# Booking GpSimd's transfers on the bus and shifting ranks by a seeded table, in the planner of a two-layer decoder kernel

## The chip, the cores and the metric

The kernel runs on one core of a Trainium2 chip. The metric is the time of one execution in microseconds (us), measured on the device. Engines are named as in the profile: PE (TensorE, matrix products), PEld (its weight loads), DVE (VectorE), ACT (ScalarE), POOL (GpSimd) and SP (SyncE, which only issues transfers here).

## The reference

Two decoder layers on 256 tokens of width 1024, all float32. Each layer has sparse attention with three branches (8 heads, 2 of keys and values) beside forgetting attention (8 heads), one output product for both, and a squared-ReLU MLP of width 4096; the norms stand before and after each half.

```python
def reference(x, w_in, ..., g_post_mlp):
    for l in range(DEPTH):                                   # 2
        h = _rms_norm(x, g_pre_mix[l])
        parts = jnp.split(h @ w_in[l], split_at, axis=-1)    # 1024 x 2848
...
        o_nsa = _nsa_mixer(...)      # compressed, selected and window branch, gated
        o_fox = _fox_mixer(...)      # softmax with summed log-sigmoid decay
        mix = jnp.concatenate([o_nsa, o_fox], axis=-1) @ w_out[l]
        x = x + _rms_norm(mix, g_post_mix[l])
        h = _rms_norm(x, g_pre_mlp[l])
        y = jnp.square(jax.nn.relu(h @ w_up[l])) @ w_down[l]
        x = x + _rms_norm(y, g_post_mlp[l])
    return x
```

## The kernel before

**Products.** A float32 product is made of three products in the rounded type float32r: both operands are split into a high part and a rest, and high·high, high·low and low·high are summed in PSUM (`mm3`). Activations lie transposed in `xT`, `aT` or `aS`. Weights come from memory in units of mostly 512 KB, and there are two ways for them. A *split* unit is loaded by SP into `wraw` (`Weights.load`, a ring of nine); ACT copies it into `whi`, and DVE subtracts `whi` from `wraw` into `wlo` (`Weights.get`; the two rings hold seven each). A *cast* unit, every second unit of `w_up` from the second column block on, 14 in a layer, goes round DVE (`Weights.cast`): a GpSimd transfer loads it rounded into the first half of a slot of `whic`, ACT writes the negative of that into the second half (`whic<-whic` in the profile), and a second GpSimd transfer adds the unrounded weights to it, which leaves the rest. The ring `whic` has three slots, so a first load waits until PE has done with the slot's former content; `CAST_LEAD` places the load 14 units ahead.

**The MLP.** Up products go to PSUM tiles `s`, 256 columns of outputs at a time; ACT and DVE make `h` of them (`h<-s`, `h<-s,h`), square and split them. Down products are made for pairs of units by a scheme of seven block products in place of eight (`Weights.pair`): DVE builds sums of weight blocks (`wsum`), which are split like weights, and seven PSUM banks (`o`, `acc`, `x`, `s`) gather the block products of thirteen pairs. Then the banks are combined once (`acc<-acc,s1`, `x<-x,s1` and so on, on DVE and ACT), and the last units are added in the plain way. At the end of a half `sandwich` normalises the result, adds it to the residual `x0` or `x1` (tokens 0 to 127 and 128 to 255), and where another product follows makes the next operand: `mg` on DVE, four PE transposes for each 512 columns (`s<-cst,mg`, `cst` holds the identity), and `xT<-s,xT` on DVE.

**What sets the order.** No engine call is made at once. A `Recorder` takes the 4876 operations with their buffers and dependences (`Recorder.add`), and a planner, `Recorder.schedule` (L325), replays them on a model of the five engines. Whenever an engine of the model is free it takes, of the operations that are ready and whose buffers are free, the one with the lowest `rank`; urgent ones go first, and two rules keep small fp32 matmuls of PE together. Ranks start as the position in the program (`key`; loads and splits have that of an earlier unit). `order` (L297) goes through four stages, the attention and the MLP of each layer, which begin at operations 0, 1095, 2464 and 3523. In each it plans, gives every operation off PE the due time that the plan's PE order sets it (`deadlines`, L269), plans again, up to four times from two starts, and keeps the ranks of the shortest plan. The order of the last plan is the order in which `emit` (L434) issues the instructions; each engine's queue then runs in that order and waits on semaphores. All instructions therefore carry the line L441 in the profile (L486 after the change).

The model's costs are nanoseconds. A transfer by SP occupies `bus` at 360 bytes per ns, and ends 900 ns after its bytes; some have an allowance on top. A GpSimd transfer does not touch `bus`: it occupies GpSimd for 1200 ns (`_cost`, L485), and what depends on it may start 5000 ns after that (`_latency`, L460).

Of the kernel before, what the change touches and what calls it, by code (L numbers as in the profile page):

```python
# [24 lines left out]
P = 128  # L25
# [8 lines left out]
LASTK = 4  # L34
LANE = 0.9
PASSES = 4
LANDING = 2500.0

SLACK, LATE = {"vector": 20, "scalar": 20}, 2000
# [146 lines left out]

class Op:
    __slots__ = ("small", "engine", "name", "args", "kw", "key", "urgent", "cost", "deps", "succs", "bufs",
                 "missing", "ready", "start", "end", "tile", "rank")


class Recorder:
# [21 lines left out]
    def add(self, engine, name, args, kw):  # L214
        if self.group is not None:
            assert engine == "tensor"
            self.group.append((name, args, kw))
            return
        op = Op()
        op.engine, op.name, op.args, op.kw = engine, name, args, kw  # L220
        op.key = len(self.ops) if self.key is None else self.key
        if self.lane is not None and self.key is None:
            op.key = self.lane + LANE * (len(self.ops) - self.lane)
        op.urgent = self.hot
        views = []
        for _, a, k in args[2] if name == "stretch" else [(name, args, kw)]:
            views += [(i == 0, v) for i, v in enumerate(a) if isinstance(v, View)]
            views += [(i in ("out", "accum_out"), v) for i, v in k.items() if isinstance(v, View)]
        op.tile = _tile(op) if engine == "tensor" else None
        op.small = engine == "tensor" and not any(v.buf.name.startswith(("whi", "wlo")) for _, v in views)  # L230
        op.cost = _cost(op, views) + SLACK.get(engine, 0)
        deps = {} if self.after is None else {self.after: -1e9}
        op.bufs = []
        for is_out, v in sorted(views, key=lambda x: x[0]):
            b, m = v.buf, v.mask()
            if b not in op.bufs:
                op.bufs.append(b)

            def against(entries):
                for o, p, q, bank in entries:  # L240
                    if o is not op and o not in deps and (
                            (bank and engine == "tensor") or
                            (p[0] < v.p[1] and v.p[0] < p[1] and (m & q).any())):
                        deps[o] = _latency(o, op)

            against(b.writes)
            entry = (op, v.p, m, is_out and b.psum and engine == "tensor")
            if is_out:
                against(b.reads)
                b.writes = [w for w in b.writes if not (  # L250
                    w[0] in deps and v.p[0] <= w[1][0] and w[1][1] <= v.p[1] and not (w[2] & ~m).any())]
                b.writes.append(entry)
            else:
                if b.psum:
                    for o, _, _, _ in b.reads:
                        if o.engine != engine and o is not op and o not in deps:
                            deps[o] = 130.0
                b.reads.append(entry)
        op.deps = deps
        for b in op.bufs:  # L260
            if not b.ops:
                self.fifo.setdefault(b.tag, []).append(b)
            b.ops += 1
        op.succs = []
        for d in deps:
            d.succs.append(op)
        self.ops.append(op)

    def deadlines(self, out):  # L269
# [14 lines left out]
        for op in reversed(out):  # L284
            d = due.get(op, t)
            cost = op.cost + LANDING if op.engine == "sync" else op.cost
            for x in op.succs:
# [9 lines left out]
    def order(self):  # L297

        for op in self.ops:
            op.rank = op.key
        done = 0
        for bound in self.stages + [len(self.ops)]:
            rest = self.ops[done:]
            best = None
            for first in ([op.rank for op in rest], [op.key for op in rest]):
                for op, rank in zip(rest, first):
                    op.rank = rank
                for i in range(PASSES + 1):  # L310
                    if i:
                        kept = [op.rank for op in self.ops[:done]]
                        self.deadlines(out)
                        for op, rank in zip(self.ops, kept):
                            op.rank = rank
                    out = self.schedule()
                    end = max(op.end for op in out)
                    if best is None or end < best[0]:
                        best = end, [op.rank for op in rest]
            for op, rank in zip(rest, best[1]):  # L320
                op.rank = rank
            done = bound
        return self.schedule()

    def schedule(self):  # L325

# [9 lines left out]
        busy = dict.fromkeys(waiting, 0.0)  # L336
        bus, tiled, loads = 0.0, (P, P), 0
# [29 lines left out]
        while events:  # L367
            t, _, released = heapq.heappop(events)
# [4 lines left out]
            for e, ops in waiting.items():  # L373
                while busy[e] <= t:
                    best = None
                    for op in ops:
                        if op.ready <= t and (best is None or (best.urgent, -best.rank) < (op.urgent, -op.rank)) and fits(op):
                            best = op
                    if best is None:
                        break  # L380
                    if e == "tensor" and best.small and not small_last and not best.urgent and t < best.ready + HOLD:
                        more = [op for op in ops if op.ready <= t and fits(op)]
                        if sum(op.small for op in more) < 2:
                            best = min((op for op in more if not op.small), key=lambda op: op.rank, default=best)
                    if e == "tensor" and small_last and not best.urgent and not best.small:
                        more = [op for op in ops if op.small and op.ready <= t and op.rank < best.rank + REACH and fits(op)]
                        best = min(more, key=lambda op: op.rank, default=best)
# [15 lines left out]
                    if e == "sync":  # L403
                        busy[e] = t + 450
                        bus = max(bus, t + 1150) + best.cost + RAMP.get(loads, 0)
                        best.end = bus + 900 + (LATE if loads >= len(FIRSTS) else 0)
                        loads += 1
                    else:
                        busy[e] = best.end = t + best.cost
                        small_last = best.small if e == "tensor" else small_last  # L410
                        if e == "tensor" and best.tile != tiled:
                            busy[e] = best.end = best.end + (tiled == (P, P)) * ENTER + (tiled != (P, P)) * LEAVE
                            tiled = best.tile
# [39 lines left out]
def _tile(op):  # L453

    up = lambda n: next(m for m in (32, 64, P) if n <= m)
    lhsT = op.args[1]
    return (P, P) if op.name == "transpose" else (up(lhsT.shape[0]), up(int(np.prod(lhsT.shape[1:]))))


def _latency(a, b):  # L460
    if a.engine == "sync":
        return 50.0
    if a.name == "dma_start":
        return 5000.0
    if a.engine == b.engine == "tensor":
        return 0.0
    if a.engine == "tensor":
        return 360.0 if b.name == "tensor_tensor_reduce" else 200.0
    if b.engine == "tensor":
        return 260.0 if a.engine == "vector" else 230.0  # L470
    return 130.0 if a.engine == "vector" else 145.0
# [13 lines left out]
def _cost(op, views):  # L485

    out = op.args[0] if op.args else op.kw["out"]
    n = int(np.prod(out.shape[1:]))
    part = 100 * (out.shape[0] < P)
    if op.engine == "gpsimd":  # L490
        if op.name == "dma_start":
            return 1200.0
        return 200 + 0.72 * n + 10 * int(np.prod(out.shape[1:-1]))
    if op.engine == "sync":
        v = views[0][1]
        return v.shape[0] * int(np.prod(v.shape[1:])) * 4 / 360.0
    if op.engine == "tensor":
        if op.name == "stretch":
            side = P // min(op.tile)
            return sum(_product(*x[:2], side) for x in op.args[2][::side])  # L500
        return _product(op.name, op.args, 1)
    if op.engine == "vector":
        if op.name == "reciprocal":
            return 60 + 6.5 * n
        if op.name == "tensor_reduce":
            n = int(np.prod(op.args[1].shape[1:]))
        fast = op.name in ("tensor_copy", "tensor_scalar", "memset") and not any(v.buf.psum for _, v in views)
        aps = sum(isinstance(v, View) for v in op.args[2:4]) if op.name == "tensor_scalar" else int(
            op.name == "scalar_tensor_tensor" and isinstance(op.args[2], View))
        return 68 + part + 64 * aps + n * (0.52 if fast else 1.04) + 10 * (op.name == "tensor_tensor_reduce")  # L510
    src = op.args[1]
    aps = sum(isinstance(op.kw.get(k), View) for k in ("bias", "scale", "accum_out"))
    return n / 1.2 + (55 if src.buf.psum else 92) + 93 * aps
# [1282 lines left out]
```

## Time and profile before

| | us |
|---|---|
| three runs | 610.91, 609.5, 611.77 |
| their median | 610.91 |
| the profiled execution | 606.49 |
| its span, first to last instruction | 604.7 |

The profiled execution is one of its own; 1.8 us of it lie outside the span. TensorE's granted clock was 0.997 of full speed in it. The rows of the page and of the timeline that carry the argument stand in the prediction. In a row of a group, the number behind the bar is the busy time, then the mean ns of one, then the idle time of that engine just ahead of them and what ended most of it.

### The profile page before, as it was taken

How to read it: one execution, taken by the hardware profiler on the slowest of the kernel's cores; microseconds unless marked ns; L12 is line 12 of the kernel's file. 1: busy time of each engine (PE TensorE's matmuls, PEld its weight loads, DVE VectorE, ACT ScalarE, POOL GpSimd, SP SyncE). 2: the span in 40 equal slices, each digit the busy share in tenths (PEclk: the TensorE clock that was granted, in tenths of full speed). 3: DMA queues.
4: the chain of work that ended last, by engine and by line, in shares of the span. 5: the costliest groups of instructions: out<-in, count | busy, mean ns of one | idle time of the engine just before them, and what ended most of it. 6: DMA issues, size and time to landing. Idle time of an engine off the chain costs nothing.

```text
span 604.7 us, 9793 instructions
## 1 busy us (share of the span) xinstructions
PE 595.4 (98%) x3322; PEld 494.7 (82%) x3322; DVE 550.6 (91%) x1187; ACT 449.3 (74%) x862; POOL 49.5 (8%) x76
## 2 busy tenths in 40 slices
PE   9999999999999999999999999999999999999995
PEld 7978887788888888887888888777888878888884
DVE  7799999989999999999699999988999989999864
ACT  7778879676977877785667769775878876878742
POOL 0000300020011111100000020001101011010000
PEclk9999999999999999999999999999999999999998
DMA  8996629688878988895247881777778878888201
GB/s 316 398 368 189 232 77 315 237 188 287 255 218 248 270 248 261 239 270 169 72 137 250 263 292 37 239 240 217 162 266 226 279 222 235 283 221 273 63 2 69
DMA packets 38850, 133.54 MB, mean 221 GB/s; under 512 B 4592, under 2 KB 4752, under 8 KB 38800
## 3 DMA queue, kind: packets, MB, share of 16 engines
q1 hardware_dynamic: 30736, 103.55, 50.3%
q0 software_dynamic: 8064, 29.36, 21.1%
q8 instruction: 26, 0.43, 0.3%
q14 instruction: 24, 0.20, 0.1%
HBM read 131.83 MB, written 1.07 MB: 220 GB/s over the span
## 4 chain that ended last, share of the span: by engine, by line
PE 86%; DVE 7%; DMA 2%; ACT 2%; issue 1%; DVEq 0%; ACTq 0%; SPq 0%
PE s L441 35%; PE acc L441 24%; PE x L441 19%; PE o L441 8%; DVE wlo L441 2%; DMA wraw<-in_w_up_dram 1%; DMA whic<-in_w_up_dram 1%; ACT whi L441 1%; DVE wsum L441 1%; DVE attn L441 1%; DVE aS L441 1%; DVE mg L441 0%; DVE h L441 0%; DVE x L441 0%; DVE quads L441 0%
## 5 line engine op out<-in xcount | busy, mean ns | idle before, releaser
L441 DVE TENSOR_TENSOR wlo<-wraw,whi 128x1024 fp32r<-128x1024 f32 (+1 forms) x160 | 177.5, 1113 | 6.8 <-ACT whi L441 6.3
L441 ACT ACTIVATE whi<-wraw 128x1024 fp32r<-128x1024 f32 (+1 forms) x160 | 153.4, 970 | 15.3 <-PE x L441 6.2
L441 PE MATMUL s<-xT,whic 128*128 128x512 f32 (+1 forms) x448 | 82.8, 337 | 0.5 <-DVE h L441 0.5
L441 PEld LDWEIGHTS s<-xT,whic 128*128 128x128 f32 x448 | 72.6, 189 | 12.1 <-DVE h L441 1.2
L441 POOL DMA_DIRECT2D whic<-in_w_up_dram x56 | 39.9, 717 | 347.7 <-ACT whic L441 120.7
L441 ACT ACTIVATE whi<-wsum 128x1024 fp32r<-128x1024 f32 x48 | 50.4, 1055 | 10.2 <-DVE wsum L441 8.9
L441 DVE TENSOR_TENSOR wlo<-wsum,whi 128x1024 fp32r<-128x1024 f32 x48 | 57.9, 1217 | 0.0
L441 PE MATMUL s<-xT,whi 128*128 128x512 f32 x224 | 55.9, 392 | 0.3
L441 PEld LDWEIGHTS s<-xT,whi 128*128 128x128 f32 x224 | 41.6, 188 | 10.5 <-DVE h L441 1.9
L441 ACT ACTIVATE attn<-attn,st 128x256 f32<-128x256 f32 (+1 forms) x96 | 42.8, 449 | 6.4 <-DVE st L441 6.3
L441 ACT ACTIVATE h<-s 128x256 f32<-128x256 f32 x56 | 21.1, 377 | 34.5 <-PE s L441 34.3
L441 PE MATMUL x<-whi,aS 128*128 128x512 f32 x112 | 43.0, 389 | 0.0
L441 PE MATMUL acc<-whi,aS 128*128 128x512 f32 x112 | 39.6, 391 | 0.0
L441 PE MATMUL x<-whi,xT 128*128 128x512 f32 x112 | 36.1, 400 | 0.2 <-DVE xT L441 0.2
L441 PE MATMUL acc<-whi,xT 128*128 128x512 f32 (+1 forms) x128 | 34.8, 348 | 0.0
L441 ACT ACTIVATE whic<-whic 128x1024 fp32r<-128x1024 f32 x28 | 29.3, 1054 | 6.8 <-DMA whic<-in_w_up_dram 6.4
L441 PE MATMUL acc<-xT,whi 128*128 128x512 f32 x128 | 34.2, 397 | 0.0
L441 PE MATMUL s<-whi,aS 128*128 128x512 f32 x96 | 34.0, 393 | 0.0
L441 DVE TENSOR_TENSOR wsum<-wraw,wsum 128x512 f32<-128x512 f32 x48 | 32.8, 683 | 0.1
L441 PEld LDWEIGHTS s<-xT,wlo 128*128 128x128 f32 x224 | 30.5, 190 | 2.2
L441 DVE TENSOR_TENSOR aS<-quads,aS 128x896 fp32r<-128x896 f32 (+3 forms) x28 | 28.3, 1009 | 3.6 <-ACT aS L441 3.6
L441 PE MATMUL s<-xT,wlo 128*128 128x256 f32 x224 | 31.2, 282 | 0.0
(235 smaller groups left out, 1340.3 us busy)
## 6 DMA issues: line engine op xcount, KB each, us to landing
wraw<-in_w_down_dram SPq DMA_DIRECT2D x64, 512.0 KB, 5.1
whic<-in_w_up_dram POOLq DMA_DIRECT2D x56, 512.0 KB, 6.4
wraw<-in_w_in_dram SPq DMA_DIRECT2D x36, 512.0 KB, 5.2
wraw<-in_w_up_dram SPq DMA_DIRECT2D x36, 512.0 KB, 4.5
wraw<-in_w_out_dram SPq DMA_DIRECT2D x16, 512.0 KB, 4.4
w<-in_cmp_w_k_dram SPq DMA_DIRECT2D x8, 512.0 KB, 5.6
w<-in_cmp_w_v_dram SPq DMA_DIRECT2D x8, 512.0 KB, 5.0
bias<-sums SPq DMA_DIRECT2D x8, 384.0 KB, 5.8
```

The source lines that it names most:

```text
L441: getattr(getattr(self.nc, op.engine), name)(*[real(v) for v in args], **{k: real(v) for k, v in kw.items()})
```

## The change

It has two parts, and the instructions stay what they are.

The booking: in the planner a GpSimd transfer now occupies GpSimd for 900 ns, takes its bytes' time on `bus`, shared with SP's transfers, from 1900 ns after its start (512 KB are 4096 · 128 / 360 = 1456 ns, an accumulating transfer is counted twice), and ends 3000 ns after them. What depends on it may start 50 ns later. For due times its cost is 6500 ns instead of 1200.

The shifts: when all passes are done, and before the last plan, each of 32 entries (seed, first, last, size) adds `size` times a normally distributed number to the rank of each operation in its range, a hundredth of that for PE's.

```diff
+CAST_HEAD, CAST_TAIL = 1900, 3000.0
+SHIFTS = ((701981142, 3587, 4092, 150),
...
+          (859060844, 573, 609, 400))
...
+        op.moved = 4096 * P / 360.0 * (1 + ("accum_op" in kw)) if engine == "gpsimd" else 0
...
             done = bound
+        for seed, a, b, size in SHIFTS:
+            self.shift(seed, a, b, size)
         return self.schedule()
+
+    def shift(self, seed, a, b, size):
+
+        for op, x in zip(self.ops[a:b], np.random.default_rng(seed).standard_normal(b - a)):
+            op.rank += size * x * (0.01 if op.engine == "tensor" else 1.0)
...
+                    elif best.name == "dma_start":
+                        busy[e] = t + 900
+                        bus = max(bus, t + CAST_HEAD) + best.moved
+                        best.end = bus + CAST_TAIL
...
     if a.name == "dma_start":
-        return 5000.0
+        return 50.0
...
         if op.name == "dma_start":
-            return 1200.0
+            return 6500.0
```

Since every engine's order comes out of the plan, the change moves instructions everywhere. Three places follow; the numbers in the names count buffers, and differ a little from kernel to kernel for the same tile.

On ACT, in the second layer's MLP, at 493 to 497 us of the profile, before:

```order
L441 ACTIVATE rl_5711<-h_5650 128x512
L441 ACTIVATE whi_5719<-wsum_5674 128x1024
L441 ACTIVATE quads_5727<-rl_5711 128x512
L441 ACTIVATE whi_5733<-wraw_5435 128x1024
L441 ACTIVATE whi_5743<-wraw_5492 128x1024
L441 ACTIVATE whic_4940<-whic_4940 128x1024
L441 ACTIVATE h_5763<-s_5717 128x256
L441 ACTIVATE whi_5768<-wraw_5512 128x512
L441 ACTIVATE aS_5775<-quads_5727 128x896
```

and now at the same place:

```order
L486 ACTIVATE rl_5713<-h_5641 128x512
L486 ACTIVATE whi_5718<-wraw_5437 128x1024
L486 ACTIVATE quads_5726<-rl_5713 128x512
L486 ACTIVATE whi_5731<-wraw_5472 128x1024
L486 ACTIVATE whi_5743<-wraw_5482 128x512
L486 ACTIVATE h_5750<-s_5715 128x256
L486 ACTIVATE whi_5763<-wsum_5710 128x1024
L486 ACTIVATE whic_4922<-whic_4922 128x1024
L486 ACTIVATE aS_5781<-quads_5726 128x896
```

The copy `whic<-whic`, which waits for GpSimd's first load of a cast unit, stood ahead of `h<-s` and stands behind it now, with one `whi` between them.

On DVE, around the combine of the second layer's banks, at 576 to 580 us of the profile, before:

```order
L441 TENSOR_TENSOR h_6490<-s_6509,h_6490 128x256
L441 TENSOR_TENSOR wlo_6543<-wraw_6341,whi_6532 128x1024
L441 TENSOR_TENSOR wlo_6555<-wraw_6380,whi_6546 128x1024
L441 TENSOR_TENSOR acc_5222<-acc_5222,s1_6559 128x512
L441 TENSOR_TENSOR aT_6573<-h2_6553,aT_6565 128x512
```

and now:

```order
L486 TENSOR_TENSOR h_6488<-s_6503,h_6488 128x256
L486 TENSOR_TENSOR wlo_6548<-wraw_6312,whi_6538 128x1024
L486 TENSOR_TENSOR acc_5229<-acc_5229,s1_6551 128x512
L486 TENSOR_TENSOR s1_6551<-s_5382,s1_6551 128x512
L486 TENSOR_TENSOR aT_6574<-h2_6545,aT_6562 128x512
```

The second of the two splits ahead of `acc` has left this place: it stands ten rows behind `acc` now (`wlo_6611<-wraw_6369`), when the combine is done.

On PE, at the boundary of the layers, at 305 to 308 us of the profile, before:

```order
L441 MATMUL o_3460<-whi_3427,xT_3451 128x512
L441 MATMUL s_3505<-cst_122,mg_3485 128x128 x4
L441 MATMUL s_3513<-cst_122,mg_3492 128x128 x4
L441 MATMUL x_3519<-whi_3290,xT_3451 128x512
L441 MATMUL x_3519<-wlo_3303,xT_3451 128x512
L441 MATMUL x_3519<-whi_3290,xT_3451 128x512 x2
```

and now:

```order
L486 MATMUL o_3463<-whi_3421,xT_3444 128x512
L486 MATMUL o_3463<-wlo_3465,xT_3444 128x512
L486 MATMUL o_3463<-whi_3421,xT_3444 128x512
L486 MATMUL s_3507<-cst_133,mg_3486 128x128 x4
L486 MATMUL o_3463<-whi_3421,xT_3444 128x512
L486 MATMUL o_3463<-wlo_3465,xT_3444 128x512
L486 MATMUL s_3518<-cst_133,mg_3493 128x128 x4
L486 MATMUL o_3463<-whi_3421,xT_3444 128x512
L486 MATMUL x_3526<-whi_3293,xT_3444 128x512
L486 MATMUL x_3526<-wlo_3333,xT_3444 128x512
L486 MATMUL acc_3529<-whi_3455,xT_3444 128x288
L486 MATMUL x_3526<-whi_3293,xT_3444 128x512 x2
```

Here `o` and `x` are PSUM banks of the second layer's first products, and the eight transposes turn the second half of the tokens. One matmul of a unit of `o` stood ahead of the transposes, and its other five behind what is shown; now three stand ahead of them, two between and one behind. On DVE that unit's split `wlo_3465` has moved ahead of the `mg` steps, and an update of `x0` behind the `xT` steps.

On SP, at the program's start, the order was: a unit, the two halves of `x0`, a unit, the constants, a unit, the two halves of `x1`, a unit. Now it is: the halves of `x0`, a unit, the first half of `x1`, a unit, its second half, the constants, two units.

More of the change, by code (lines that the diff above doesn't have):

```diff
@@ L36 @@
 PASSES = 4
+CAST_HEAD, CAST_TAIL = 1900, 3000.0
+SHIFTS = ((701981142, 3587, 4092, 150),
+          (891084246, 1875, 2268, 150),
+          (136102123, 2395, 2490, 400),
+          (100171639, 300, 554, 150),
+          (602402177, 3120, 3183, 1000),
+          (479715909, 2967, 3000, 2500),
+          (446931837, 3329, 3407, 400),
+          (130812457, 178, 265, 1000),
+          (231451964, 3457, 3547, 1000),
+          (327370210, 1562, 2486, 400),
+          (640343220, 1657, 2050, 150),
+          (519233017, 3188, 3301, 2500),
+          (1020438500, 2276, 2427, 150),
+          (882894196, 389, 1170, 150),
+          (298925097, 387, 437, 150),
+          (266265942, 494, 537, 2500),
+          (95822864, 3359, 4132, 400),
+          (616631038, 3416, 3989, 400),
+          (882980751, 582, 623, 1000),
+          (379167277, 3289, 3368, 1000),
+          (1013096470, 325, 368, 1000),
+          (48202901, 4257, 4844, 400),
+          (65264732, 2222, 2288, 400),
+          (958946402, 1958, 2118, 1000),
+          (443481147, 3372, 3402, 400),
+          (195006458, 1662, 2260, 150),
+          (454856537, 1913, 2284, 150),
+          (762260381, 3290, 3363, 150),
+          (698749673, 2064, 2112, 1000),
+          (67036745, 487, 590, 1000),
+          (848283408, 620, 679, 150),
+          (859060844, 573, 609, 400))
 LANDING = 2500.0
@@ L188 @@
     __slots__ = ("small", "engine", "name", "args", "kw", "key", "urgent", "cost", "deps", "succs", "bufs",
-                 "missing", "ready", "start", "end", "tile", "rank")
+                 "missing", "ready", "start", "end", "tile", "rank", "moved")
 class Recorder:
```

## The prediction

> **What bounds the kernel now.** I began with the page, whose rows follow: the span, each engine's busy time, the chain that ended last, then two groups of instructions and one DMA issue.
>
> ```profile
> span 604.7 us, 9793 instructions
> PE 595.4 (98%) x3322; PEld 494.7 (82%) x3322; DVE 550.6 (91%) x1187; ACT 449.3 (74%) x862; POOL 49.5 (8%) x76
> ...
> PE 86%; DVE 7%; DMA 2%; ACT 2%; issue 1%; DVEq 0%; ACTq 0%; SPq 0%
> ...
> L441 ACT ACTIVATE whic<-whic 128x1024 fp32r<-128x1024 f32 x28 | 29.3, 1054 | 6.8 <-DMA whic<-in_w_up_dram 6.4
> ...
> whic<-in_w_up_dram POOLq DMA_DIRECT2D x56, 512.0 KB, 6.4
> ```
>
> PE is busy for 595.4 of 604.7 us and makes 86% of the chain. Instructions are the same after the change, so only gaps between matmuls can be won or lost. A pipelined matmul's busy time hides such gaps; I read them from starts. In the timeline (start, busy time, engine, operation, tile, count, and the idle time with its releaser in brackets) an undisturbed stretch looks like this:
>
> ```profile
> 591.60 0.62 PE L441 MATMUL x<-whi,aT 128*128 128x512 f32 x2
> 592.05 0.39 PE L441 MATMUL x<-wlo,aT 128*128 128x512 f32 x1
> ```
>
> Two matmuls of 512 columns take 0.45 us from start to start: the pace is 0.227 us each. What a step takes beyond its pace is lost. I went through PE's timeline for steps over pace and compared the large ones with the order of before and of the change. Four kinds of gap are touched.
>
> **Gap 1, late cast data.** The first place is at 495 us: a GpSimd load of an odd `w_up` unit, and who waits for it:
>
> ```profile
> 488.47 0.55 POOL L441 DMA_DIRECT2D whic<-in_w_up_dram  x1 [0.84 <-PE s L441]
> ...
> 495.39 1.06 ACT L441 ACTIVATE whic<-whic 128x1024 fp32r<-128x1024 f32 x1 [0.43 <-DMA whic<-in_w_up_dram]
> 496.33 0.39 PE L441 MATMUL x<-whi,aS 128*128 128x512 f32 x1
> ...
> 496.75 0.42 DVE L441 TENSOR_TENSOR h<-s,h 128x256 f32<-128x256 f32 x1 [0.47 <-ACT h L441]
> 497.24 0.50 PE L441 MATMUL s<-xT,whic 128*128 128x512 f32 x1 [0.52 <-DVE h L441]
> ```
>
> ACT stands 0.43 us for the transfer, copies for 1.06 us, and only then does its `h`, for which DVE's `h` and then PE wait. PE's step is 497.24 − 496.33 = 0.91 us, so 0.68 is lost. A second place:
>
> ```profile
> 527.76 1.06 ACT L441 ACTIVATE whic<-whic 128x1024 fp32r<-128x1024 f32 x1 [1.19 <-DMA whic<-in_w_up_dram]
> ...
> 533.34 0.39 PE L441 MATMUL x<-whi,aS 128*128 128x512 f32 x1
> 533.86 0.50 PE L441 MATMUL s<-xT,whi 128*128 128x512 f32 x1
> ```
>
> ACT stood 1.19 us and stayed behind; PE's step five microseconds on is 0.52, so 0.29 is lost. Together 0.97 us.
>
> **The change part by part: the booking.** The planner used to let a cast land 5000 ns after a 1200 ns issue, without the bus; it now books transfer time on the bus shared with SP and expects a later landing where the bus is full. In the order of the change nearly every ACT copy `whic<-whic` stands 9 to 27 PE instructions later behind its load, and at 495 us behind `h` and one `whi`, not ahead of them. The landing's median is 6.4 us by the page; 12 PE steps are 12 × 0.227 = 2.7 us, more than the 1.19 us that ACT waited at worst. The consumer on PE still stands 80 or more PE instructions behind its copy, 80 × 0.227 = 18 us, so a copy 5 us later delays no matmul. I take all 0.97 us as gained; the bounds are 0 and 0.97.
>
> At eight places GpSimd's queue has the next cast's first load ahead of the current cast's accumulating load. The accumulate then goes out some 2 us later (the ring slot's wait of 0.84 us above and the next issue); beside an 18 us lead that is covered. Uncovered, each would cost what it is late, 2 us.
>
> The Trainium skill, "DMA: Bandwidth & Descriptors", section "🔬 Anatomy of one DMA — SWDGE (gpsimd) path", fits a GpSimd DMA as a fixed 2.0 us plus bytes over 436e3. An estimate by it gives 512 KB some 3.2 us; the load of 488.47 would then have been there before ACT came to it, gap 1 would be no matter of DMA, and the sum below would be smaller by 0.97. The rows say otherwise, 488.47 to 495.39 with ACT waiting, and they decide.
>
> **The shifts, gap 2: the combine at 577 us.** The last MLP product is combined while DVE also splits weights:
>
> ```profile
> 576.81 1.23 DVE L441 TENSOR_TENSOR wlo<-wraw,whi 128x1024 fp32r<-128x1024 f32 x1 [0.24 <-ACT whi L441]
> ...
> 577.21 1.11 PE L441 MATMUL s<-xT,wlo 128*128 128x256 f32 x8
> 577.95 0.69 DVE L441 TENSOR_TENSOR acc<-acc,s 128x512 f32<-128x512 f32 x1
> 578.70 0.50 PE L441 MATMUL acc<-whi,aT 128*128 128x512 f32 x1 [0.38 <-DVE acc L441]
> ...
> 586.03 0.69 DVE L441 TENSOR_TENSOR aT<-h,aT 128x512 fp32r<-128x512 f32 x1 [2.03 <-ACT aT L441]
> ```
>
> The eight 256-column matmuls, at about half the pace, 0.12 each, would release PE at 577.21 + 0.96 = 578.17; it starts at 578.70, so 0.53 is lost behind a split that `acc` had to let pass. In the change one of the two splits stands behind the whole combine and `acc` comes directly after the first. I take 0.53; bounds 0 and 0.53. The split moved away is taken by PE only with this last `aT`, before which DVE idles for 2.03 us: room for its 1.23.
>
> **Gap 3: the layer boundary at 305 us.** The transposes of the new activations against the undisturbed four at 299 us:
>
> ```profile
> 299.25 0.60 PE L441 MATMUL s<-cst,mg 128*128 128x128 f32 x4
> 299.61 0.48 PE L441 MATMUL acc<-wlo,aT 128*128 128x512 f32 x1
> ...
> 305.60 1.47 PE L441 MATMUL s<-cst,mg 128*128 128x128 f32 x8
> 306.49 0.74 DVE L441 SCALAR_TENSOR_TENSOR x<-m,rsqrt,x 128x512 f32<-128x512 f32 x1
> 306.96 0.50 PE L441 MATMUL x<-whi,xT 128*128 128x512 f32 x1
> 307.30 0.40 PE L441 MATMUL x<-wlo,xT 128*128 128x512 f32 x1
> 307.89 0.50 PE L441 MATMUL x<-whi,xT 128*128 128x512 f32 x1 [0.20 <-DVE xT L441]
> ```
>
> Four take 0.36 us, so eight should take 0.72 and took 1.36; the two steps behind them are 0.34 and 0.59. Lost: 0.64 + 0.11 + 0.36 = 1.11. The change puts five more matmuls `o<-whi` and `o<-wlo` of the old `xT` half ahead of and between the transposes, 5 × 0.227 = 1.14 us of work while DVE prepares. They need their `wlo` earlier: that split (1.23, as at 576.81) now stands in DVE's chain, and one `x` update (0.74, the row of 306.49) has left it, so DVE comes 0.49 later. What is left to wait is 1.11 + 0.49 − 1.14 = 0.46; the gain is 0.65. Bounds: a loss of 0.49 if the fillers hide nothing, a gain of 1.11 if the split falls in idle time.
>
> **Gap 4: the gains at 276 us.** The product of two norms' gains stands ahead of `h`:
>
> ```profile
> 276.11 1.22 DVE L441 TENSOR_TENSOR gains<-gains 128x1024 f32<-128x1024 f32 x1
> 277.19 0.39 PE L441 MATMUL x<-whi,aS 128*128 128x512 f32 x1
> 277.25 0.42 DVE L441 TENSOR_TENSOR h<-s,h 128x256 f32<-128x256 f32 x1
> 277.72 0.50 PE L441 MATMUL s<-xT,whi 128*128 128x512 f32 x1
> ```
>
> PE's step is 0.53, lost 0.30. Now `h` stands ahead of the gains. I take 0.30; bounds 0 and 0.30.
>
> **What is added.** First, runs of small fp32 matmuls between weight matmuls: the order has 91, before 85. The step behind such a run was 0.34 at 306.96, 0.11 over pace, so six cost 0.7 us at most; 0 if they fall where PE waits anyway. I take 0.6. Second, the start. SP's queue now has `x`'s quarters and the constants ahead of the weight units that they stood behind, on a bus that is full:
>
> ```profile
> 10.00:24.00 14.00, 14.00 (x86) 12.70 (x85) 10.31 (x33) 11.95 (x32) 0.00 (x0) 1.00 1.03 396
> ```
>
> Moved past 256 KB a unit comes 0.66 us later at 396 GB/s, past two of them 1.3. The unit that is split first is needed late:
>
> ```profile
> 12.84 0.69 ACT L441 ACTIVATE whi<-wraw 128x576 fp32r<-128x576 f32 x1
> 16.71 0.42 PE L441 MATMUL acc<-whi,xT 128*128 128x288 f32 x2
> ```
>
> A lead of 3.9 us covers 1.3 us for this one; the units behind it I cannot follow so closely, since ACT's order moves there too. Bounds 0 and 1.3, taken 0.5.
>
> Sum: −(0.97 + 0.53 + 0.65 + 0.30) + 0.6 + 0.5 = −1.35, say −1.4 us. The profiled execution of 606.49 us would become 605.1. It lies 4.4 us under the median of the runs without the profiler, 610.91 us; I carry the difference over: **609.5 us**, −0.2%. About 0.5% (3.05 us) is what a measurement of this kernel can tell from no change, so this is within it.
>
> **Rivals.** *Faster by more than 0.5%.* The gaps close as bounded, gap 3 wholly, neither the runs nor the start cost anything, and another combine like that of 577 closes too:
>
> ```profile
> 279.78 1.00 PE L441 MATMUL s<-xT,wlo 128*128 128x256 f32 x7
> ...
> 281.13 0.50 PE L441 MATMUL acc<-whi,aT 128*128 128x512 f32 x1 [0.35 <-DVE acc L441]
> ```
>
> Seven at 0.12 end at 280.61, so 0.52 is lost. Sum −(0.97 + 0.53 + 1.11 + 0.30 + 0.52) = −3.4, or 607.5 us. For it: shifts by up to 2500 in rank touch far more places than the four, and each small stall of 0.1 us may go as well. Against it: here the order looks the same, ACT sets the combine, and small stalls can also come. 0.27.
>
> *Slower: DVE becomes the bound in the attention stages.* There it has no room:
>
> ```profile
> 45.00:65.00 20.00, 20.00 (x149) 16.77 (x149) 19.62 (x63) 16.56 (x35) 1.54 (x4) 1.00 0.77 238
> ```
>
> DVE is busy for 19.62 of 20 us there, and PE follows it. More than half of the 32 shifts lie in the attention parts, and they move DVE and ACT by a hundred times what they move PE. If a split of 1.23 us comes ahead of a softmax step that PE needs next, and PE has no filler, that time is lost. It decides once DVE's queue behind the split is longer than PE's lead at that place, about a microsecond. At two places per layer it costs 4 × 1.23 = 4.9, with the sum −1.4 + 4.9 = +3.5: 614.4 us. Against it: PE is busy throughout this window, DVE's queue or not, so it has filler. 0.12.
>
> *The casts do not matter.* If PE's losses at 497 and 533 us come from ACT's other work, they stay: −1.4 + 0.97 = −0.4, or 610.5 us. It lies within the forecast's own bounds; its chance of 0.15 is part of the forecast's.
>
> **How the numbers follow.** My forecast, with the casts' rival in it, has 0.61; faster 0.27; slower 0.12. Its own bounds: gains of 0 to 2.9 and costs of 0 to 2.5 (gap 3's loss 0.5, runs 0.7, start 1.3), hence 608.0 to 613.4 at the extremes; these don't come all at once. The range reaches down to the faster case, 607.5, with a microsecond of small stalls more, and up to no gain with half of the costs, 610.91 + 1.25: 606.5 to 612.2. Some 0.08 lies below and 0.12 above.
>
> **What would show it.** Gap 1: ACT's idle time for `whic` falls from 6.4 us to under 2, and no step over 0.4 us stands at the two `h`. Gap 2: `acc<-whi,aT` follows the eight `s<-xT,wlo` at 0.96 us. Gap 3: from the first transpose to the second `x<-whi,xT`, after subtracting the fillers, under 2 us. Gap 4: steps of 0.23 around the last `h` of the first layer's MLP. The start: PE's first `acc<-whi,xT` of 288 columns within 0.5 us of 16.71. I am wrong if PE's steps in the attention windows grow by more than a microsecond in sum, or if cast operands come late (PE waiting for ACT or DMA `whic`).

## The result: faster by 8.4 us, and the profile after

Five runs of the change lay between 600.96 and 602.34 us, median 601.77; five of before between 606.86 and 611.77, median 610.91. The ratio is 0.9863 (95% interval 0.9829 to 0.9897), some 8.4 us; the medians lie 9.1 us apart. The forecast was 609.5, range 606.5 to 612.2: the sign was right, the size far off.

The profiled execution went from 606.49 to 602.34 us, so the two profiles differ by 4.15 us. The other 5.0 us between the medians are not in them: before's profiled execution lay 4.4 us under its median, the change's 0.6 above its own.

The page of the change, the same rows as of before:

```profile
span 600.6 us, 9803 instructions
PE 591.8 (99%) x3322; PEld 494.3 (82%) x3322; DVE 550.2 (92%) x1187; ACT 450.1 (75%) x862; POOL 47.5 (8%) x76
...
PE 95%; DVE 2%; ACT 1%; DMA 1%; issue 1%; DVEq 0%; ACTq 0%
...
L486 ACT ACTIVATE whic<-whic 128x1024 fp32r<-128x1024 f32 x28 | 29.3, 1049 | 6.2 <-DMA whic<-in_w_up_dram 6.1
...
whic<-in_w_up_dram POOLq DMA_DIRECT2D x56, 512.0 KB, 7.6
```

The chain now leads through PE alone for 95% of the span. ACT still waits 6.1 us for cast data, which was 6.4: against the forecast that wait has not gone. When PE starts comparable work in both profiled executions, by the first or last matmul of a kind:

| PE's work | before | change | difference |
|---|---|---|---|
| first `acc<-whi,xT`, the start | 16.71 | 16.25 | −0.46 |
| first `s<-xT,whi`, MLP of layer 1 | 141.53 | 139.98 | −1.55 |
| seventh `acc<-wlo,aT`, end of layer 1's MLP | 296.52 | 294.40 | −2.12 |
| first `acc<-xT,whi` of layer 2 | 334.50 | 331.33 | −3.17 |
| first `s<-xT,whi`, MLP of layer 2 | 438.06 | 435.04 | −3.02 |
| last `acc<-whi,aT` | 597.72 | 593.57 | −4.15 |

The start and layer 1's attention give 1.55, its MLP 0.57, the boundary 1.05, layer 2's attention −0.15, its MLP 1.13. Now the places of the prediction, in the timeline of the change. Gap 2, the combine:

```profile
573.65 0.69 DVE L486 TENSOR_TENSOR acc<-acc,s 128x512 f32<-128x512 f32 x1
573.71 1.12 PE L486 MATMUL s<-xT,wlo 128*128 128x256 f32 x8
...
574.66 0.40 PE L486 MATMUL acc<-whi,aT 128*128 128x512 f32 x1
```

`acc` is done before the eight matmuls are; they take 0.95 us from start to start, and nothing is lost. Gap 3, the boundary:

```profile
303.91 0.60 PE L486 MATMUL s<-cst,mg 128*128 128x128 f32 x4
...
304.82 0.60 PE L486 MATMUL s<-cst,mg 128*128 128x128 f32 x4
305.18 0.47 PE L486 MATMUL o<-whi,xT 128*128 128x512 f32 x1
...
305.49 0.39 PE L486 MATMUL x<-whi,xT 128*128 128x512 f32 x1
...
306.08 0.63 PE L486 MATMUL x<-whi,xT 128*128 128x512 f32 x2
```

From the first transpose to the second `x<-whi,xT` pass 2.17 us, with 0.72 of transposes, 5 × 0.227 of matmuls and 0.13 of a short one in them: 0.19 is lost, where it was 1.11. Gap 4:

```profile
275.04 0.41 DVE L486 TENSOR_TENSOR h<-s,h 128x256 f32<-128x256 f32 x1
...
275.38 1.21 DVE L486 TENSOR_TENSOR gains<-gains 128x1024 f32<-128x1024 f32 x1
...
276.12 0.39 PE L486 MATMUL x<-whi,aS 128*128 128x512 f32 x1
276.35 1.98 PE L486 MATMUL s<-xT,whi 128*128 128x512 f32 x8
```

The step is 0.23: closed. At gap 1's two places there is no step either, but the profile of the change has another of the same kind, the largest in it, at 487 us:

```profile
483.44 1.06 ACT L486 ACTIVATE whic<-whic 128x1024 fp32r<-128x1024 f32 x1 [2.27 <-DMA whic<-in_w_up_dram]
...
487.14 0.36 ACT L486 ACTIVATE h<-s 128x256 f32<-128x256 f32 x1
...
487.33 1.22 DVE L486 TENSOR_TENSOR wlo<-wsum,whi 128x1024 fp32r<-128x1024 f32 x1
...
487.71 0.39 PE L486 MATMUL s<-whi,aS 128*128 128x512 f32 x1
488.47 0.42 DVE L486 TENSOR_TENSOR h<-s,h 128x256 f32<-128x256 f32 x1
...
488.94 0.73 PE L486 MATMUL s<-xT,whi 128*128 128x512 f32 x2 [0.84 <-DVE h L486]
```

The copy waits 2.27 us, everything behind it on ACT is late, DVE lets a split of 1.22 us pass ahead of `h`, and PE's step is 1.23: 1.00 us lost. So the cast waits moved rather than went, and yet the medians differ by twice what the profiles do.

### The profile page after: what moved, and what is told of

It is laid out like the page before. It is cut to its first block, busy times and chain, and to the rows that moved or that the text cites. A ratio compares the mean times of both kernels' runs of the same rounds, so it can differ in the third digit from the quotient of the medians.

```text
span 600.6 us, 9803 instructions
## 1 busy us (share of the span) xinstructions
PE 591.8 (99%) x3322; PEld 494.3 (82%) x3322; DVE 550.2 (92%) x1187; ACT 450.1 (75%) x862; POOL 47.5 (8%) x76
## 4 chain that ended last, share of the span: by engine, by line
PE 95%; DVE 2%; ACT 1%; DMA 1%; issue 1%; DVEq 0%; ACTq 0%
PE s L486 39%; PE acc L486 26%; PE x L486 20%; PE o L486 9%; DVE wlo L486 1%; DMA first<-in_first_dram 1%; ACT whi L486 1%; DVE wsum L486 0%; ACT aS L486 0%; DVE h L486 0%; DVE aS L486 0%; DVE quads L486 0%; ACT rl L486 0%; ACT h L486 0%; DVE x L486 0%
## 5 line engine op out<-in xcount | busy, mean ns | idle before, releaser
L486 PE MATMUL s<-xT,whic 128*128 128x512 f32 (+1 forms) x448 | 85.0, 336 | 0.0
L486 PEld LDWEIGHTS s<-xT,whic 128*128 128x128 f32 x448 | 73.4, 189 | 11.2
L486 PE MATMUL acc<-whi,aS 128*128 128x512 f32 x112 | 41.4, 392 | 0.0
```

Source lines behind the costliest of these rows:

```text
L486: getattr(getattr(self.nc, op.engine), name)(*[real(v) for v in args], **{k: real(v) for k, v in kw.items()})
```

## The experiments

First all runs in one table. "Waits for h" are PE's weight loads of `s` waiting for DVE's `h` in the profiled execution, "waits for cast" ACT's `whic` copy waiting for its transfer: sum in us and number. Ratios are to runs of before on the same chip.

| run | median us | lowest to highest | ratio (95%) | waits for h | waits for cast |
|---|---|---|---|---|---|
| profile of before | | | | 3.1, 7 | 6.4, 8 |
| profile of the change | | | | 2.1, 3 | 6.1, 5 |
| e0_before | 610.38 | 606.83 to 614.81 | 1.0016 (0.9989 to 1.0042) | 5.7, 10 | 10.0, 13 |
| e1_booking | 607.43 | 605.66 to 608.07 | 0.995 (0.9931 to 0.9969) | 4.8, 4 | 6.7, 4 |
| e2_shifts | 628.64 | 627.24 to 630.12 | 1.03 (1.0277 to 1.0323) | 11.9, 13 | 11.8, 13 |
| e3_seeds | 607.96 | 606.87 to 613.16 | 0.9978 (0.9954 to 1.0002) | 4.5, 7 | 4.5, 4 |
| e4_late | 615.14 | 613.84 to 616.24 | 1.008 (1.0051 to 1.0109) | 11.2, 17 | 1.6, 2 |
| e6_after_late | 606.62 | 605.85 to 608.35 | 0.9946 (0.9924 to 0.9968) | 4.0, 10 | none |
| e7_mlp | 604.34 | 601.49 to 605.46 | 0.9894 (0.9851 to 0.9938) | 1.4, 2 | 4.9, 7 |
| e8_att | 603.54 | 602.63 to 603.77 | 0.9885 (0.9851 to 0.9919) | 3.3, 5 | 5.5, 5 |
| e9_behind_h | 605.89 | 604.94 to 607.07 | 0.9902 (0.9866 to 0.9937) | 2.1, 7 | none |
| e10_h_first | 601.34 | 601.03 to 603.06 | 0.9834 (0.9795 to 0.9873) | 1.3, 5 | 2.4, 4 |
| e11_after | 601.52 | 600.96 to 603.09 | 0.9832 (0.9796 to 0.9867) | 1.0, 2 | 5.1, 6 |
| e12_after_behind_h | 601.60 | 601.11 to 601.87 | 0.9853 (0.9825 to 0.988) | 1.1, 3 | none |
| e13_booking_behind_h | 603.17 | 602.76 to 603.45 | 0.9879 (0.9851 to 0.9906) | 1.4, 1 | none |
| e14_seeds_behind_h | 607.78 | 606.65 to 610.22 | 0.9961 (0.994 to 0.9983) | 3.0, 4 | 0.8, 1 |

### Before once more

The file is unchanged.

> The kernel before, unchanged, once more. Question: the time of before lay between 606.9 and 611.8 us in its runs, of the change between 601.0 and 602.3. Theory of late transfers: before waits for transfers at its casts, its start and its weights, so its runs scatter with the landings; a profiled execution near 610 us then shows more idle time for DMA whic or wraw on ACT and PE steps over pace at those places, at the same granted clock. Rival, the clock: an execution near 610 us has a granted clock lower by some 0.5% and the same steps. Expected 606 to 612 us, ratio 0.997 to 1.003.

Its profiled execution took 608.53 us, 2.0 more than the first one, at a granted clock of 0.998 against 0.997, so the clock is not it. One place shows what is: a copy in layer 1's MLP, with the `h` behind it, first in the profile of before:

```profile
260.17 1.06 ACT L441 ACTIVATE whic<-whic 128x1024 fp32r<-128x1024 f32 x1
261.13 0.36 ACT L441 ACTIVATE h<-s 128x256 f32<-128x256 f32 x1
...
262.46 0.39 PE L441 MATMUL s<-wlo,aS 128*128 128x512 f32 x1
262.69 0.62 PE L441 MATMUL s<-xT,whic 128*128 128x512 f32 x2
```

and the same instructions in the profile of the repetition:

```profile
261.21 1.06 ACT L441 ACTIVATE whic<-whic 128x1024 fp32r<-128x1024 f32 x1 [1.75 <-DMA whic<-in_w_up_dram]
...
262.11 0.39 PE L441 MATMUL s<-wlo,aS 128*128 128x512 f32 x1
262.18 0.36 ACT L441 ACTIVATE h<-s 128x256 f32<-128x256 f32 x1
...
263.06 0.72 PE L441 MATMUL s<-xT,whic 128*128 128x512 f32 x2 [0.56 <-DVE h L441]
```

With the transfer there in time PE's step is 0.23; with 1.75 us of waiting it is 0.95, 0.72 over pace. The repetition has another 0.71 like it at 562 us, and 0.66 at 535 where it was 0.30. These three make 1.8 of the 2.0 us. The time of before depends on how its casts happen to land, and one profiled execution shows one such draw. For the slowest executions this is not all: of before's on record, those with a granted clock of 0.994 or less took 614.1 us and more, those with 0.996 or more 606.8 to 614.8. None of the slowest was profiled.

### The two parts alone, and other seeds

Booking without the shifts, shifts without the booking, and the whole with other random numbers:

```diff
 # e1_booking, in order()
-        for seed, a, b, size in SHIFTS:
-            self.shift(seed, a, b, size)
 # e2_shifts: the three places of the booking as before
-            return 6500.0
+            return 1200.0
...
 # e3_seeds, in shift()
-        ... np.random.default_rng(seed) ...
+        ... np.random.default_rng(seed + 1) ...
```

> Only the booking; the table of shifts is not applied. Its order has the change's start on SP, its combine (one split ahead of acc) and its fillers at the layer boundary, so these come from the booking. Theory that the booking carries the gain: 602 to 604.5 us, ratio 0.986 to 0.990. Rival, that the selected shifts carry it: 606 to 609 us, ratio 0.993 to 0.998.

> Only the shifts, on the old booking. Its order has before's start, two splits ahead of acc and no fillers. Theory that the booking carries the gain: 608 to 612 us, ratio 0.996 to 1.002. Rival, that the shifts carry it whatever ranks they are added to: 603 to 606 us, ratio 0.987 to 0.993.

> The whole change with every seed of the table raised by one: other numbers in the same ranges and sizes. If the shifts help by being these numbers, this is slower than the change by 2 us or more, 604 to 609 us, and slower than the booking alone. If the numbers do not matter, it is within 1 us of the change, 601 to 603 us.

The booking alone has the start, the boundary's fillers and the combine's order, which the prediction had put down to the shifts but for the start, and gives 0.5%, some 3 us: the rival of the first expectation. In its profile gap 3 and the combine of layer 1 are closed, but gap 2 still loses 0.41 us and gap 4, where the gains stand ahead of `h` as before, now 1.00. The selected shifts bring the larger rest. But not any shifts do: on the old booking the same table costs 3%, and the one other set of numbers that was tried gives away what the booking gains, or nearly (the interval reaches 1.0002). Most of the 18 us of `e2_shifts` go in four places, at 147, 274, 464 and 540 us, where PE stands for 2.1 to 3.1 us and has a lower clock for a while after. The timeline and the windows (length, busy time of PE, PEld, DVE, ACT and POOL, granted clock, DMA share, GB/s) show the last of them:

```profile
540.38 4.43 PE L482 MATMUL s<-xT,whic 128*128 128x512 f32 x16 [3.08 <-DVE h L482]
```

```profile
540.40:543.40 3.00, 3.00 (x7) 2.42 (x8) 2.42 (x4) 0.95 (x1) 0.00 (x0) 0.51 0.95 283
543.80:547.00 3.20, 3.20 (x20) 2.79 (x19) 0.43 (x1) 1.63 (x3) 0.55 (x1) 1.00 0.60 161
```

PE waits 3.08 us for one `h`, ahead of which DVE has two splits, and then runs at half the clock for three microseconds more. The table that gains on one plan does harm on the other.

### The copies four rows later

A pass over the finished order moves each of the 28 ACT copies behind the fourth ACT instruction after it, on before and on the change:

```diff
+        for op in [o for o in out if o.engine == "scalar" and o.bufs[0].name == "whic"]:
...
+            for _ in range(4):
+                j = next(k for k in range(j + 1, len(out)) if out[k].engine == "scalar")
...
+            out[i:j + 1] = rest + moved
```

> The order of before, with each of the 28 ACT copies whic<-whic moved four ACT instructions later and nothing else (its accumulating load follows it where it stood ahead). Theory that before loses by copies that stand in ACT's queue ahead of a late landing: ACT's idle time for whic falls from 6 to 10 us to under 3, the steps over pace at h in the MLP go, 604 to 607 us, ratio 0.990 to 0.996, runs closer together than before's 6 us. Rival, that the rest of the order makes the difference: 608.5 to 611 us, ratio 0.998 to 1.002.

> The change, with each ACT copy whic<-whic four ACT instructions later. The change's profile has one large step left in the MLP, at 487.7 us (1.0 us over pace), behind a copy that waited 2.3 us. If that is all there is, 600 to 601.5 us, about 1 us under the change. Rival, the copy pushes other ACT work behind it into PE's way at its new place: 602 to 604 us.

Both fell. On before ACT's wait for casts went from 6.4 to 1.6 us, as meant, and the runs came together (2.4 us apart, against 8.0 of the repetition), but the time rose by 0.8%. The list of waits of `e4_late` (engine and line, releaser, sum in us, times, longest) says why:

```profile
PEld s L456 <- DVE h L456: 11.2, 17, 1.7
...
ACT whic L456 <- DMA whic<-in_w_up_dram: 1.6, 2, 1.3
```

PE waits 17 times for `h`. A copy is 1.06 us of ACT wherever it stands, and four rows on it stands in ACT's unbroken work ahead of the next `h`. At the two largest steps, 1.63 and 1.51 us, it stands directly ahead of it; the first of them:

```profile
228.68 1.04 ACT L456 ACTIVATE whic<-whic 128x1024 fp32r<-128x1024 f32 x1
...
229.62 0.36 ACT L456 ACTIVATE h<-s 128x256 f32<-128x256 f32 x1
...
230.50 0.74 PE L456 MATMUL s<-xT,whi 128*128 128x512 f32 x2 [1.24 <-DVE h L456]
```

At 182 us, with a step of 0.75, it stands five rows ahead: there it delays a `whi`, DVE's split waits 0.86 us for that, and DVE comes late to its `h`. On the change (`e6_after_late`) PE waits ten times for `h`, and once, at 147 us, 0.99 us for a cast's transfer itself. A new theory: what counts is how much ACT and DVE do ahead of an `h` that PE needs next; a late transfer is one way in which that grows.

### Which stages the shifts serve

```diff
         for seed, a, b, size in SHIFTS:
+            if 1095 <= (a + b) // 2 < 2464 or (a + b) // 2 >= 3523:     # e8_att: if not (...)
                 self.shift(seed, a, b, size)
```

> The booking with only those entries of the table whose middle lies in an MLP stage. In the profiles the change gains over the booking alone 3.1 of 3.3 us in the two MLP stages. If each entry does its work in its own place: 601.5 to 603.5 us. Rival, the table works only as a whole, since each entry was drawn on the plan that the others make: 605 to 609 us.

> The booking with only those entries whose middle lies in an attention stage. If each entry does its work in its own place: 606.5 to 608 us, like the booking alone (607.4). Rival, the table works only as a whole: the MLP stages come out at random, 604 to 610 us.

Neither expectation holds as it stood. The MLP's entries give 604.34, the attention's 603.54 us, so either half brings more than half of what the table does beyond the booking (by the ratios, whose intervals are 0.4% to either side, about half or more). The attention's half does so in the MLP: of the 1.95 us by which PE's last matmul comes earlier than with the booking alone, 1.2 arise in layer 1's MLP and 0.45 in layer 2's. An entry moves what comes after it, too: in the MLPs PE's order is that of the booking alone, those of ACT and DVE are not. So the table's entries can't all be read as local repairs. Some can: with the MLP's half gaps 2 and 4 are closed, with the attention's half gap 4 still loses 1.00 us.

### The copies behind the next h

The same pass, but to directly behind the next `h<-s` of ACT, where one stands within six instructions (22 of 28):

```diff
+            act = [k for k in range(i + 1, len(out)) if out[k].engine == "scalar"][:6]
+            j = next((k for k in act if self.is_h(out[k], "scalar")), None)
+            if j is not None:
...
+                self.put(out, [op] + ([acc] if out.index(acc) < j else []), j)
```

> The order of before, with each ACT copy whic<-whic that has an h<-s within the next six ACT instructions moved directly behind that h, 22 of 28; nothing else. Four rows later the copies waited little for their transfer but came before the next h, and PE waited for 18 h in place of 10. Theory that a copy costs by the h behind it: the wait for the transfer and the h it delays both go, PE waits for fewer than 10 h, 604 to 607.5 us, ratio 0.990 to 0.997, and the runs lie within 4 us. Rival, any later copy costs, by its later accumulating load or by the ACT work behind it: 611 to 616 us.

The ratio is 0.9902, from this move of 22 instructions alone, and the runs lie 2.1 us apart where before's beside them lie 7.3. At the place of 496 us:

```profile
496.17 0.36 ACT L464 ACTIVATE h<-s 128x256 f32<-128x256 f32 x1
496.43 1.05 ACT L464 ACTIVATE whic<-whic 128x1024 fp32r<-128x1024 f32 x1
497.50 0.42 DVE L464 TENSOR_TENSOR h<-s,h 128x256 f32<-128x256 f32 x1
...
498.20 0.39 PE L464 MATMUL x<-whi,aS 128*128 128x512 f32 x1
...
498.43 1.75 PE L464 MATMUL s<-xT,whic 128*128 128x512 f32 x7
```

The copy starts without waiting and holds no `h` up; PE goes on at pace. The steps of gap 1 are gone; those of gaps 2 to 4 stand as before (0.55, 1.1 in sum and 0.31 us), and the combine of layer 1 (0.52). With `e4_late` this makes a pair: neither waits for its casts to speak of, the copies stand a few rows apart, and 9 us lie between the medians (1.8% by the ratios). The gain shows in the medians only: the profiled execution here, 607.07 us, is the slowest of its six, and before's was 606.49. It is without the 0.97 us of gap 1, but at 33 us a weight unit loaded by SP came late, and PE lost 1.38 us there. So casts are not the only transfers that can be late.

Beside it, DVE's `h` put ahead of the one split at the change's two steps:

```diff
+        for n in (4, 20):      # the copies at 168 and 483 us
...
+            self.put(out, [long], j)      # wlo<-wsum behind h<-s,h
```

> The change, with DVE's h<-s,h put ahead of the one wlo<-wsum that stands before it at two places, 171.5 and 487.3 us of its profile, where PE's steps are 0.33 and 1.00 us over pace; nothing else. Theory that an instruction of 1.2 us ahead of h is the price of such a step: both steps go, 1.0 to 1.3 us less than the change beside it, 600 to 601 us. Rival, the step follows ACT's copy alone, or the delayed wlo is missed by PE next: within 0.5 us of the change.

> The change unchanged, for the runs beside it on the same chip: 601 to 602.5 us.

No difference, 601.34 and 601.52. The profile of the unchanged kernel tells why this could show little: the copy of 483.44 waited 0.44 us in that execution, not 2.27, and the step of 1.00 us behind it is not there. It was a draw as well. The other step, 0.33 us at 173 us, stands in that profile and is gone in `e10_h_first`, but six runs don't show so little. The test says nothing against the price of the step of 1.00 us, which only one of two profiled executions of the change has.

### Does the table gain by the same thing?

The pass of `e9_behind_h` on the change, on the booking alone and on the other seeds:

> The change, with 22 copies moved directly behind the next h as before. Eight of the change's copies stand directly ahead of an h, yet PE waits for two or three h only. If the selected shifts gain by giving the copies places that suffice, the move brings nothing more: 600.5 to 603 us. Rival, there is still time in them: 598 to 600 us.

> The booking alone, no shifts, with 22 copies moved directly behind the next h. Theory that the selected shifts gain over the booking (607.4 against 601.8 us) by where the copies and the long splits stand against h: 602 to 604.5 us, most of the gain without any shift. Rival, the shifts gain elsewhere (attention, many small steps): 606 to 608 us.

> The other draw of the table (608.0 us) with 22 copies moved directly behind the next h. Same theory: 602 to 605 us; rival: 606.5 to 609 us.

On the booking alone the copies' place brings 607.43 to 603.17 us (by the ratios 0.71%, 4.3 us), without any shift. On the change it brings nothing: with the selected table the copies no longer matter. It isn't their number ahead of an `h` that tells: directly ahead stand 6 in before, 12 in the booking alone and 8 in the change.

The change has 1.5 us more than `e13_booking_behind_h`, and the profiles say where. Gap 4 is open in `e13_booking_behind_h`, with a step of 277.47 − 276.11 = 1.36 us, 1.13 over pace:

```profile
275.87 1.22 DVE L507 TENSOR_TENSOR gains<-gains 128x1024 f32<-128x1024 f32 x1
...
276.11 0.39 PE L507 MATMUL x<-whi,aS 128*128 128x512 f32 x1
277.00 0.42 DVE L507 TENSOR_TENSOR h<-s,h 128x256 f32<-128x256 f32 x1
...
277.47 1.90 PE L507 MATMUL s<-xT,whi 128*128 128x512 f32 x7 [0.97 <-DVE h L507]
```

Gap 2 is open there too, with 0.42 us; in the change both are closed. That is read from one profile of each; no run changes these two places alone.

The other seeds stay at 607.78. Their loss lies elsewhere: against the change's profile this one's first `s<-xT,whi` is 1.7 us later in layer 1, so after the attention, in which PE stands for 1.38 us at 101 us and ACT has a `whi` of 1.06 us ahead of the `prX<-s` that PE waits for. Three steps of 0.5 to 1.1 us come at the end of that layer's MLP, 2.6 in sum, gap 4 among them. No version here beats the change by more than its runs spread.

## Why the prediction was wrong

- **The carry-over to the median failed**, the largest mistake. The prediction read 4.4 us between profile and median as a constant. But the profiled execution was a lucky draw: none of the 87 others of before on record is under 606.8 us. What differs from draw to draw is mostly late casts. PE's steps behind copies that waited cost 0.97 us in the first profile and 2.67 in the repetition; without them 605.5 and 605.9 us are left, and 605.89 is the median of `e9_behind_h`, in which no copy waits for its cast. Before's runs spread over 5 to 8 us, those of `e9_behind_h`, `e12_after_behind_h` and `e13_booking_behind_h` over 0.7 to 2.1. The change's own copies do wait, and its runs spread over 1.4 to 2.1: what costs is not the wait by itself but one that reaches an `h` that PE needs. Of the 9.1 us between the medians 5.0 lie between profile and median. That casts make most of them is inferred from these sums, since no execution of before near its median was profiled.
- **Gap 1 was mis-sized.** 0.97 us was one execution's draw; moving the copies of before shows about 6 us (0.9902). The mechanism was named rightly, copy ahead of `h`, but the cure was taken for a later copy, so that ACT would not wait; `e4_late` shows that copies which hardly wait can cost more. The order near 495 us was quoted with the copy ahead of `h` and behind it; where the other copies stand against theirs was not counted. That a later copy delays no matmul did not hold either where copies were moved further: see the 0.99 us of `e6_after_late`.
- **Gaps 2 and 4 were right in size**, 0.53 and 0.30, and gap 3 gave 0.92, not 0.65. The combine of layer 1, expected to stay, closed as well (279.11 follows eight matmuls from 278.16). Which part of the change does it was partly wrong: the prediction put all three under the shifts, but gap 3 and the combine of layer 1 close with the booking alone. Gap 2 falls to 0.41 there and gap 4 grows to 1.00, and both close with the table's entries for the MLP.
- **The added costs were not there.** The start was booked at +0.5 and gave −0.46, runs of small matmuls at +0.6 and show nothing: the steps from the last matmul of such a run to the weight matmul behind it sum to 10.4 us in before's trace (85 runs) and to 9.6 in the change's (91). With the attention of layer 1 (1.55 − 0.46 = 1.1 us gained, expected 0; 0.9 of it with the booking alone) this is 2.7 us, about the difference between −1.4 and −4.15 of the profiles. Gap 3 and the combine of layer 1 gave 0.8 more than forecast, and the new step at 488 us took 1.0 back.
- **The slower rival** did not come with this table. Something near it came with others: the other seeds lose 1.7 us by the end of layer 1's attention, and the table on the old booking has splits ahead of an `h` and costs 3%. The prediction treated the shifts as a thing of known effect at four places; their sum over hundreds of moves depends on which numbers were picked, as drawing others shows.

What stays open: what gained in the attention of layer 1, which entries of the table put `h` ahead of the gains, what an execution of before near its median looks like, and what spreads the runs of `e14_seeds_behind_h` over 3.6 us though it hardly waits for casts; its slowest, 610.22 us, has a granted clock of 0.994, the others 0.996 to 0.999.

## What to carry to other kernels

Take two or three profiles of the same kernel before pricing a wait for a transfer: a step that isn't there in one execution can cost 0.7 or 1.0 us in the next, and a gap between the profiled execution and the median is a term to explain, not to carry over. In an in-order queue, a long instruction that doesn't matter by itself is priced by the short one behind it: put the copy behind the hand-over that the busy engine waits for, not simply later. A table of random shifts belongs to the plan that it was selected on; with other base costs it did harm.

## What the runs showed of the hardware

After PE had stood for 3.08 us its granted clock was 0.51 for the next 3 us, as shown above. After 2.28 us, and about a microsecond of work, it did the same, with 0.50, from 465 to 468 us of `e2_shifts`:

```profile
463.93 0.50 PE L482 MATMUL x<-whi,aS 128*128 128x512 f32 x1 [2.28 <-ACT aS L482]
```

```profile
465.00:468.00 3.00, 3.00 (x8) 2.30 (x7) 2.19 (x6) 2.29 (x5) 0.00 (x0) 0.50 0.97 169
```

So such a stall costs some 1.5 us more behind it: the sixteen matmuls from 540.38 us take 4.27 us until the next one starts, sixteen undisturbed ones 2.76 (from 179.69 us of before); behind the other stall seven steps from 465.04 us take 2.99 us, at pace 1.59. The Trainium skill, "TensorE: Matmul & The Clock Gate", section "🔬 Part 1: The HAM clock gate (the "warmup" mystery)", has half rate after an idle window of some 3.4 us and release after as much busy time; the half rate and the three microseconds agree, while here less idle time, 2.28 us, was enough. Stalls of about 1 us, as at 488 us of the change, were followed by no such loss: the clock was 1.00 from 489 to 492 us.
